# The scaled input of the projections: from x laid out twice and factors spread by matmuls, in place of transposes

## The chip, the cores and the metric

The kernel runs on one core of one Trainium2 chip. The metric is the device time of one execution in microseconds. Before the change three runs took 4046.52 to 4047.17, with a median of 4046.59.

The engines are called as in the profile: PE does matrix products and transposes, PEld is its loading of the stationary operand, DVE, ACT and POOL work on tiles element by element, and SP issues nearly all DMAs.

## The reference

One layer of a streaming encoder on 4096 tokens of 1024 features, in float32. The part that matters here is its first step, the RMS norm of the tokens and the projection:

```python
def rmsnorm(x, w):
    xf = x.astype(jnp.float32)
    y = xf * lax.rsqrt(jnp.mean(xf * xf, axis=-1, keepdims=True) + EPS)
    return (y * w.astype(jnp.float32)).astype(x.dtype)

a = rmsnorm(h, attn_norm_w[i])
proj = (a @ w_in[i]).astype(f32)          # 1024 -> 3584 columns
sb_q, sb_k, sb_v, hg_q, hg_f, hg_i, hg_g = jnp.split(proj, ...)
# blocks of 128 tokens: stick-breaking attention on sb_q, sb_k, sb_v (8 heads of 64)
# a gated linear recurrence on hg_* (4 heads of 128), out projection, residual
# routed experts, per-layer embeddings, a last RMS norm
```

Each token is divided by its own root mean square. The weights of the norm belong to features and are multiplied into `w_in`.

## The kernel before

`mix_phase` (line 162) is the first of five phases and ends its first part at some 770 us. It cuts the tokens into 16 chunks of 256 (`CH`) and works through jobs: A for chunks 0 to 15, which project v, k and q and do the attention, then B, twice over the chunks, for the recurrence. The change touches the jobs A only.

**Products.** Each fp32 product of the projections is done as three products of rounded halves (`mm3`, lines 103 to 105). Both operands are therefore split: into a rounded part `h` and the rest `l`. For the tokens these are the tiles `ATh` and `ATl`, features on partitions and tokens in the row.

**Preparation of a chunk** (`prep`, line 181). `xload` (line 178) brings x with tokens on partitions, two tiles `xin` of 128x1024. `stat` lets ACT square and sum each token (line 189), DVE works out one over the root in Newton's steps (`rsqrt_newton`, lines 66 to 74, tiles `xnr` and `xrs`), and POOL (DVE in chunk 0) multiplies the two tiles by it (line 194). Then four calls `tr(g)` each transpose four blocks of 128x128 on PE against the identity into PSUM (line 202, tile `xtp`); ACT copies that to SBUF (line 205), tile `on`; ACT makes the rounded part (line 207) and DVE the rest (line 208). The copy also goes to DRAM (`atd`, line 209), from where the jobs B read it again.

**Order.** All engines work in the order in which the code issues (the schedule is a manual one). `weave` (line 45) merges lists of steps by a position from 0 to 1 in the job. The job of chunk c has as its main list 24 steps of projections: eight for v (`tok_major`), eight for k and eight for q (`col_major`). Beside it run the attention of chunk c-1 and the preparation of chunk c+1. The table `PREP` has the positions of the latter: `stat` at 0.3 and the four `tr` at 0.5, 0.568, 0.636 and 0.704 (for chunk 1, in the first job, 0.44 and 0.62 onward). `xload` of chunk c+2 is at 0.931.

**Attention** (`attn`, line 398) goes head by head through `stage(h)`. On PE a pair of heads gets its scores (`zz`, lines 404 and 406). Then, for head h: two sigmoids on ACT (`sn` and `sp`, lines 412 and 413), a scan on DVE (line 415, `aP`), a product on POOL (line 418, `a`), a small update on DVE (line 421, `pcar`). The head two back is transposed on PE (line 427) and masked by DVE (line 429) into `aTs`, and the head three back is multiplied with v on PE (`avm`, lines 440 and 441), with `aTs` as the stationary operand. `aTs` has one buffer, `a` three, `on` two. When the keys of heads 0 and 4 begin to be projected, ACT also moves the last columns of the old keys (`carry`, line 359, `kst`).

**The start.** Before the first job, DVE and ACT split the weights of v and k (lines 150 and 151), 512 columns each, in steps of 128 features, while x and the weights come in. DVE's copy of the first results of v (line 353) stands behind these.

Of the kernel before, what the change touches and what calls it, by code (L numbers as in the profile page):

```python
# [7 lines left out]
F32 = mybir.dt.float32  # L8
# [4 lines left out]
AF = mybir.ActivationFunctionType  # L13
# [79 lines left out]
PREP = [0.3, 0.5, 0.068, 0.44, 0.62, 0.049, 0.931]  # L93
# [68 lines left out]
def mix_phase(tc, nc, x, anw, w_in, lbd, mix, qd, kd, vd, atd, C, flag, wp, atp, next_weights, filler):  # L162
    with tc.tile_pool(name="gw", bufs=1) as gw, tc.tile_pool(name="r4", bufs=3) as r4p, \
# [17 lines left out]
        def prep(c):  # L181
            st = {}

            def stat():
                ms = sm.tile([P, BPC], F32, name="xms", tag="xms")
                at = halves(atp)
                junk = at[1].rearrange("p k t -> p (k t)")
                for b in range(BPC):
                    nc.scalar.activation(junk[:, b * D:(b + 1) * D], X[c][b], AF.Square, accum_out=ms[:, b:b + 1])
                r = sm.tile([P, BPC], F32, name="xrs", tag="xrs")  # L190
                rsqrt_newton(nc, sm, r, ms, 1.0 / D, EPS, "xnr")
                eng = nc.gpsimd if c else nc.vector
                for b in range(BPC):
                    eng.tensor_scalar(X[c][b], X[c][b], r[:, b:b + 1], 0.0, op0=OP.mult, op1=OP.add)
                AT[c] = at

            def tr(g):
                ps = ptp.tile([P, 2, CH], F32, name="xtp", tag="tp")
                for j in range(2):
                    for b in range(BPC):  # L200
                        k = g * 2 + j
                        nc.tensor.transpose(ps[:, j, b * P:(b + 1) * P], X[c][b][:, k * P:(k + 1) * P], C["id"])
                tag = "on" if c else ("on", "a", "sn", "sp")[g]
                f = tm.tile([P, 2, CH], F32, name=tag, tag=tag, bufs=TB.get(tag))
                nc.scalar.activation(f, ps, AF.Copy)
                h = AT[c][0][:, 2 * g:2 * g + 2, :]
                nc.scalar.activation(h, f, AF.Copy)
                nc.vector.tensor_tensor(AT[c][1][:, 2 * g:2 * g + 2, :], f, h.bitcast(F32), op=OP.subtract)
                nc.sync.dma_start(atd[c][:, g * 512:(g + 1) * 512], f.rearrange("p k t -> p (k t)"))
            if c == 1:  # L210
                return [(PREP[3], stat)] + [(PREP[4] + PREP[5] * g, lambda g=g: tr(g)) for g in range(4)]
            return [(PREP[0], stat)] + [(PREP[1] + PREP[2] * g, lambda g=g: tr(g)) for g in range(4)]

# [30 lines left out]

        def two(t):
            return t.rearrange("p (k n) -> p k n", k=2)
        ws = {n: W.steps(n, cols[n], nw, [lambda t=t: two(t) for t in ts]) for n, ts in (("v", spare), ("k", more))}
        first[0][1]()
        for f in ws["v"][:2]:
            f()  # L250
        for _, f in first[1:]:
            f()
# [431 lines left out]
        for i, (kind, hp, c) in enumerate(jobs):  # L684
# [7 lines left out]
            if i + 1 < len(jobs):  # L692
                nk, _, n_c = jobs[i + 1]
                if nk == "A":
                    sides.append(prep(n_c))
                    if n_c + 1 < NCH:
                        sides.append([(PREP[6], lambda n_c=n_c: xload(n_c + 1))])
                else:
                    sides.append(atload(n_c, kind == "B" and i > NCH))
# [1156 lines left out]
def trunk(tc, x, p, attn_norm_w, w_in, sb_norm_w, hg_lower_bounds, hg_norm_w, w_out, ffn_norm_w, w_group_router,  # L1856
# [3 lines left out]
    with tc.tile_pool(name="dram", bufs=1, space=DRAM) as dp, tc.tile_pool(name="c", bufs=1) as cp, tc.manual_schedule():  # L1860
# [15 lines left out]
        with ExitStack() as early_e, ExitStack() as early:  # L1876
# [3 lines left out]
            with tc.tile_pool(name="AT", **right) as at1, tc.tile_pool(name="W", bufs=5, side="right") as w5:  # L1880
# [10 lines left out]
                W, mT, pre = mix_phase(tc, nc, x[0], attn_norm_w[0], w_in[0], hg_lower_bounds, mix, qd, kd, vd, atd, C, R["aflag"],  # L1891
# [35 lines left out]
```

## Time and profile before

| | |
|---|---|
| profiled execution | 4046.34 us |
| its span | 4044.6 us |
| median of three runs | 4046.59 us |
| PE busy | 3985.5 us, 99% |
| DVE, ACT, POOL busy | 68%, 46%, 21% |
| mean granted clock of PE | 0.996 of full speed |
| 375 to 425 us, a steady stretch of the jobs A: busy of 50 us | PE 49.95, DVE 35.41, ACT 30.28, POOL 12.70 |
| same stretch, mean share of the DMA engines | 0.24 |

The span goes from the first to the last instruction; the profiled execution has 1.7 us around it. Matmuls are pipelined, and their ends are modelled, so the time that one takes is best read from the starts of the next ones. In a timeline each row has the start in us from the start of the span, the duration, the engine, the line, the operation with what it writes and reads, and in brackets how long its engine sat idle before it and who ended that. "x2" or "x4" are that many instructions merged into one row; a whole fp32 product is recorded as two.

### The profile page before, as it was taken

What the parts mean: (1) busy time and instruction counts of PE and PEld (TensorE: products, weight loads), DVE (VectorE), ACT (ScalarE), POOL (GpSimd) and SP (SyncE); (2) the same over time, 40 slices, a digit from 0 to 9 for tenths busy, and PEclk for the clock granted to TensorE, in tenths of its full rate; (3) what the DMA queues carried; (4) which work ended last, traced back from release to release, by engine and by line L of the source; (5) the groups of instructions that cost most, each with busy time, mean ns of one, the idle gap of its engine ahead of it and who ended that gap; (6) DMA issues with size and microseconds to landing.
All of it is one profiled execution on the core that took longest, in us unless ns stands there. A gap on an engine that the chain in (4) does not pass through costs nothing. (4 is left out here: it accounts for less than half of the span.)

```text
span 4044.6 us, 70031 instructions
## 1 busy us (share of the span) xinstructions
PE 3985.5 (99%) x26635; PEld 3607.3 (89%) x26635; DVE 2747.5 (68%) x5871; ACT 1851.5 (46%) x3345; POOL 839.4 (21%) x1075
## 2 busy tenths in 40 slices
PE   8999999999999999999999989999999999999998
PEld 7999999999999899997888879989889999987887
DVE  6777777787777778775666656655555566657776
ACT  6666666643333333323222344545555555554443
POOL 1322222222222222220111110100000000004564
PEclk9999999999999999999999999999999999999999
DMA  4222222321211112115454486776767777776654
GB/s 151 84 84 84 84 85 85 108 60 42 61 48 56 50 40 69 45 41 196 145 162 145 149 238 196 220 215 206 228 211 236 233 239 238 224 235 246 235 212 151
DMA packets 482386, 590.33 MB, mean 146 GB/s; under 512 B 33882, under 2 KB 332890, under 8 KB 482042
## 3 DMA queue, kind: packets, MB, share of 16 engines
q1 hardware_dynamic: 459370, 510.70, 40.1%
q0 software_dynamic: 22672, 75.07, 5.2%
q8 instruction: 212, 3.47, 0.4%
q14 instruction: 132, 1.08, 0.1%
HBM read 423.86 MB, written 161.81 MB: 145 GB/s over the span
## 5 line engine op out<-in xcount | busy, mean ns | idle before, releaser
L103 PE MATMUL pj<-ATh,W 128*128 128x256 f32 x2048 | 610.0, 298 | 4.0 <-DVE v L353 4.0
L103 PE MATMUL pg<-dxth,wph 128*128 128x256 f32 (+6 forms) x2048 | 602.9, 294 | 2.0 <-ACTq L1650 2.0
L105 PE MATMUL pg<-dxth,wpl 128*128 128x256 f32 (+6 forms) x2048 | 588.7, 287 | 0.0
L104 PE MATMUL pg<-dxtl,wph 128*128 128x256 f32 (+6 forms) x2048 | 588.2, 287 | 0.0
L105 PE MATMUL pj<-ATh,W 128*128 128x256 f32 x2048 | 580.5, 283 | 0.0
L1310 DVE TENSOR_TENSOR wpl<-wraw,wph 128x2048 fp32r<-128x2048 f32 x192 | 439.3, 2289 | 207.1 <-ACT wph L1299 206.5
L104 PE MATMUL pj<-ATl,W 128*128 128x256 f32 x2048 | 579.8, 283 | 0.0
L103 PE MATMUL pj<-W,ATh 128*128 128x512 f32 x1308 | 524.0, 401 | 0.3 <-ACT mixin L1219 0.3
L104 PE MATMUL pj<-W,ATh 128*128 128x512 f32 x1308 | 510.1, 390 | 0.0
L105 PE MATMUL pj<-W,ATl 128*128 128x512 f32 x1280 | 501.0, 391 | 0.0
L103 PEld LDWEIGHTS pj<-ATh,W 128*128 128x128 f32 x2048 | 392.7, 192 | 7.8 <-issue 4.4
L104 PEld LDWEIGHTS pj<-ATl,W 128*128 128x128 f32 x2048 | 393.3, 192 | 0.1
L105 PEld LDWEIGHTS pj<-ATh,W 128*128 128x128 f32 x2048 | 392.0, 191 | 0.0
L103 PEld LDWEIGHTS pg<-dxth,wph 128*128 128x128 f32 x2048 | 385.3, 188 | 4.4 <-ACTq L1650 2.4
L104 PEld LDWEIGHTS pg<-dxtl,wph 128*128 128x128 f32 x2048 | 386.2, 189 | 1.4
L105 PEld LDWEIGHTS pg<-dxth,wpl 128*128 128x128 f32 x2048 | 386.0, 188 | 0.0
L1299 ACT ACTIVATE wph<-wraw 128x2048 fp32r<-128x2048 f32 x192 | 365.8, 1905 | 0.0
L1525 POOL DMA_INDIRECT dxr<-mnd,idx x79 | 84.9, 1074 | 1077.3 <-PE dtp L1536 1034.8
L105 PEld LDWEIGHTS pj<-W,ATl 128*128 128x128 f32 x1280 | 240.3, 188 | 53.0
L104 PEld LDWEIGHTS pj<-W,ATh 128*128 128x128 f32 x1308 | 246.4, 188 | 45.6 <-DVE W L151 0.2
L103 PEld LDWEIGHTS pj<-W,ATh 128*128 128x128 f32 x1308 | 246.3, 188 | 44.7 <-ACT mixin L1219 0.5
L418 POOL TENSOR_TENSOR a<-sp,aP 128x512 f32<-128x512 f32 x128 | 153.8, 1206 | 560.0 <-DVE pcar L421 296.7
(440 smaller groups left out, 8763.0 us busy)
## 6 DMA issues: line engine op xcount, KB each, us to landing
wraw<-in_w_exp_gate_dram SPq DMA_DIRECT2D x128, 512.0 KB, 4.1
wraw<-in_w_exp_up_dram SPq DMA_DIRECT2D x128, 512.0 KB, 5.3
wraw<-in_w_exp_down_dram SPq DMA_DIRECT2D x64, 1024.0 KB, 5.1
a<-atd SPq DMA_DIRECT2D x128, 256.0 KB, 3.1
yd<-dyo SPq DMA_DIRECT2D x108, 256.0 KB, 3.1
xin<-in_x_dram SPq DMA_DIRECT2D x32, 512.0 KB, 4.7
cxin<-in_x_dram SPq DMA_DIRECT2D x32, 512.0 KB, 7.9
h1d<-h SPq DMA_DIRECT2D x32, 512.0 KB, 3.0
```

What stands on the lines that cost most here:

```text
L103: nc.tensor.matmul(out, ph, rh, start=first, stop=False)
L104: nc.tensor.matmul(out, ph, rl, start=False, stop=False)
L105: nc.tensor.matmul(out, pl, rh, start=False, stop=last)
L418: nc.gpsimd.tensor_tensor(a, sp, pt[:, 1:513], op=OP.mult)
L1299: self.nc.scalar.activation(h, t, AF.Copy)
L1310: self.nc.vector.tensor_tensor(l, t, h.bitcast(F32), op=OP.subtract)
L1525: nc.gpsimd.indirect_dma_start(out=t, out_offset=None, in_=mnd, in_offset=bass.IndirectOffsetOnAxis(ap=idx[:, e * NB + s:e * NB + s + 1], ...
```

## The change

The host gives x a second time, as `xt`, cut into chunks with features on partitions. `xload` and the Squares stay, since the sum over a token's features is still made from the first layout. `stat` no longer multiplies x. It writes each token's factor along a row of 128: two tiles of 128x128 (identity times zero, plus the factor), on POOL, in chunk 0 on DVE. `spread_r` multiplies these on PE with the identity, two whole fp32 products, which gives the 256 factors along the row on all partitions, and ACT copies them from PSUM to SBUF. Then `scaled(g)`, four times, multiplies a quarter of `xt` by them, on POOL (in chunk 0 on DVE); ACT's rounding, DVE's subtraction and the DMA to `atd` follow as before. The factors use the halves of the second `xin` tile. `get(j)` loads the two halves of `xt`; they take turns with `xin` in the ring `r4` of three buffers.

The positions change too: `get(0)` at 0.02, `stat` at 0.2 (was 0.3), `get(1)` at 0.23, `spread_r` at 0.46, `scaled` at the old places of `tr`. In chunk 1 they are 0.3, 0.44, 0.47, 0.58 and 0.62 onward.

```diff
-PREP = [0.3, 0.5, 0.068, 0.44, 0.62, 0.049, 0.931]
+PREP = [0.02, 0.2, 0.5, 0.068]
+PREP1 = [0.3, 0.44, 0.62, 0.049]
+XLOAD = 0.931
...
+            def get(j):
+                t = r4p.tile([P, 4, CH], F32, name="xtr", tag="r4") if c else gw.tile([P, 4, CH], F32, name="xtr", tag=("s4", "ql1")[j])
+                nc.sync.dma_start(t, xt[c][:, 4 * j:4 * j + 4, :])
+                st[j] = t
...
+                st["r"], st["b"] = (X[c][1][:, j * 512:j * 512 + CH] for j in range(2))
                 eng = nc.gpsimd if c else nc.vector
                 for b in range(BPC):
-                    eng.tensor_scalar(X[c][b], X[c][b], r[:, b:b + 1], 0.0, op0=OP.mult, op1=OP.add)
+                    eng.tensor_scalar(st["r"][:, b * P:(b + 1) * P], C["id"], 0.0, r[:, b:b + 1], op0=OP.mult, op1=OP.add)
                 AT[c] = at
 
-            def tr(g):
-                ps = ptp.tile([P, 2, CH], F32, name="xtp", tag="tp")
-                for j in range(2):
-                    for b in range(BPC):
-                        k = g * 2 + j
-                        nc.tensor.transpose(ps[:, j, b * P:(b + 1) * P], X[c][b][:, k * P:(k + 1) * P], C["id"])
+            def spread_r():
+
+                ps = ptp.tile([P, CH], F32, name="xrb", tag="tp", padded_shape=[P, 512])
+                for b in range(BPC):
+                    s = slice(b * P, (b + 1) * P)
+                    nc.tensor.matmul(ps[:, s], st["r"][:, s], C["id"], start=True, stop=True)
+                nc.scalar.activation(st["b"], ps, AF.Copy)
+
+            def scaled(g):
                 tag = "on" if c else ("on", "a", "sn", "sp")[g]
                 f = tm.tile([P, 2, CH], F32, name=tag, tag=tag, bufs=TB.get(tag))
-                nc.scalar.activation(f, ps, AF.Copy)
-                h = AT[c][0][:, 2 * g:2 * g + 2, :]
+                h, l = (t[:, 2 * g:2 * g + 2, :] for t in AT[c])
+                eng = nc.gpsimd if c else nc.vector
+                eng.tensor_tensor(f, st[g // 2][:, 2 * (g % 2):2 * (g % 2) + 2, :],
+                                  st["b"].rearrange("p (o t) -> p o t", o=1).broadcast_to([P, 2, CH]), op=OP.mult)
                 nc.scalar.activation(h, f, AF.Copy)
-                nc.vector.tensor_tensor(AT[c][1][:, 2 * g:2 * g + 2, :], f, h.bitcast(F32), op=OP.subtract)
+                nc.vector.tensor_tensor(l, f, h.bitcast(F32), op=OP.subtract)
                 nc.sync.dma_start(atd[c][:, g * 512:(g + 1) * 512], f.rearrange("p k t -> p (k t)"))
...
+            a = np.ascontiguousarray(a.reshape(NCH, CH, KC, P).transpose(0, 3, 2, 1))
+            arrays["in_xt_dram"] = a
```

Three places in the new order follow. Lines are those of the file that the rows belong to, so the same operation has two numbers.

The first is in a steady chunk, on ACT and POOL, around head 6 of the attention. ACT before: the sigmoids of head 6, the copy and rounding of the first quarter, the copying of keys, the sigmoids of head 7.

```order
L412 ACTIVATE sn<-z 128x512
L413 ACTIVATE sp<-z 128x512
L205 ACTIVATE on<-xtp 128x512
L207 ACTIVATE ATh<-on 128x512
L359 ACTIVATE kst<-kst 128x2x128 x2
L412 ACTIVATE sn<-z 128x512
L413 ACTIVATE sp<-z 128x512
```

ACT now, at the same place:

```order
L431 ACTIVATE sn<-z 128x512
L432 ACTIVATE sp<-z 128x512
L220 ACTIVATE ATh<-on 128x512
L378 ACTIVATE kst<-kst 128x2x128 x2
L431 ACTIVATE sn<-z 128x512
L432 ACTIVATE sp<-z 128x512
```

POOL now, from head 5 on; before, only products of line 418 stood here. The `on` that ACT rounds is the first of the four multiplies.

```order
L437 TENSOR_TENSOR a<-sp,aP_260 128x512
L437 TENSOR_TENSOR a<-sp,aP_259 128x512
L218 TENSOR_TENSOR on<-xtr,xin 128x512
L437 TENSOR_TENSOR a<-sp,aP_260 128x512
L218 TENSOR_TENSOR on<-xtr,xin 128x512 x3
```

The source of `on` moved from a copy on ACT itself to POOL, behind the product of head 6.

The second place is on DVE in the same chunk, around head 3: the scan, the update and the mask of head 1, and Newton's steps (the first and last two of which are shown). Before:

```order
L415 SCALAR_TENSOR_TENSOR aP_272<-sn,areset 128x512
L421 TENSOR_TENSOR pcar<-pcar,aP_272 128x2
L429 TENSOR_TENSOR aTs<-aT,amask 128x512
L66 TENSOR_SCALAR xnr_v<-xms 128x2
L67 TENSOR_SCALAR xnr_i<-xnr_v 128x2
```

Now:

```order
L73 TENSOR_TENSOR xnr_t<-xnr_t,xnr_v 128x2
L74 SCALAR_TENSOR_TENSOR xrs<-xnr_t,xrs 128x2
L434 SCALAR_TENSOR_TENSOR aP_260<-sn,areset 128x512
L440 TENSOR_TENSOR pcar<-pcar,aP_260 128x2
L448 TENSOR_TENSOR aTs<-aT,amask 128x512
```

Newton's steps moved from behind head 3's scan to in front of it.

The third place is on DVE at the start, between Newton's steps for chunk 0 and the weights. Before:

```order
L194 TENSOR_SCALAR xin<-xin,xrs 128x1024 x2
L151 SCALAR_TENSOR_TENSOR W<-ATh,anw,W 128x512 x4
L208 TENSOR_TENSOR ATl<-on,ATh 128x512
L208 TENSOR_TENSOR ATl<-a,ATh 128x512
L208 TENSOR_TENSOR ATl<-sn,ATh 128x512
L208 TENSOR_TENSOR ATl<-sp,ATh 128x512
L151 SCALAR_TENSOR_TENSOR W<-ATl,anw,W 128x512 x4
```

Now:

```order
L202 TENSOR_SCALAR xin<-ident,xrs 128x128 x2
L153 SCALAR_TENSOR_TENSOR W<-ATh,anw,W 128x512 x4
L218 TENSOR_TENSOR on<-xtr,xin 128x512
L221 TENSOR_TENSOR ATl<-on,ATh 128x512
L218 TENSOR_TENSOR a<-xtr,xin 128x512
L221 TENSOR_TENSOR ATl<-a,ATh 128x512
L218 TENSOR_TENSOR sn<-xtr,xin 128x512
L221 TENSOR_TENSOR ATl<-sn,ATh 128x512
L218 TENSOR_TENSOR sp<-xtr,xin 128x512
L221 TENSOR_TENSOR ATl<-sp,ATh 128x512
L153 SCALAR_TENSOR_TENSOR W<-ATl,anw,W 128x512 x4
```

The multiplies stand between the splits on one engine, and each split of DVE needs ACT's rounding of the multiply just ahead of it.

## Rows read from the trace of the kernel before

**Rows 1.** Part 1 of the page: busy us, share of the span, instructions, by engine
```profile
PE 3985.5 (99%) x26635; PEld 3607.3 (89%) x26635; DVE 2747.5 (68%) x5871; ACT 1851.5 (46%) x3345; POOL 839.4 (21%) x1075
```
**Rows 2.** Waits of PE and its weight loads, first 770 us: total, times, longest
```profile
PE xtp L202 <- DVE xin L194: 10.5, 1, 10.5
PE pj L103 <- DVE v L353: 4.0, 1, 4.0
PE xtp L202 <- POOL xin L194: 0.9, 1, 0.9
...
PEld o L440 <- DVE aTs L429: 4.5, 14, 0.9
```
**Rows 3.** Timeline of PE in chunk 8: start, duration, engine, line, operation
```profile
428.82 0.33 PE L440 MATMUL o<-v,aTs 128*128 128x64 f32 x2
...
439.33 0.61 PE L202 MATMUL xtp<-ident,xin 128*128 128x128 f32 x4
439.70 0.36 PE L103 MATMUL pj<-ATh,W 128*128 128x256 f32 x1
...
446.28 0.33 PE L440 MATMUL o<-v,aTs 128*128 128x64 f32 x2
...
450.44 0.60 PE L202 MATMUL xtp<-ident,xin 128*128 128x128 f32 x4
450.88 0.60 PE L427 MATMUL aT<-ident,a 128*128 128x128 f32 x4
```
**Rows 4.** Timeline of PE, six whole fp32 products of 128x128 in a row
```profile
1030.42 0.39 PE L631 MATMUL o<-hvg,fqs 128*128 128x128 f32 x2
...
1031.67 0.48 PE L103 MATMUL pj<-W,ATh 128*128 128x512 f32 x1
```
**Rows 5.** Timeline of ACT in chunk 8
```profile
423.67 1.06 ACT L189 ACTIVATE ATl<-xin 128x1024 fp32r<-128x1024 f32 x1
...
438.59 0.60 ACT L412 ACTIVATE sn<-z 128x512 f32<-128x512 f32 x1
...
440.61 0.63 ACT L207 ACTIVATE ATh<-on 128x512 fp32r<-128x512 f32 x1
...
441.76 0.57 ACT L412 ACTIVATE sn<-z 128x512 f32<-128x512 f32 x1
```
**Rows 6.** Timeline of DVE in chunk 8
```profile
426.80 0.31 DVE L66 TENSOR_SCALAR xnr_v<-xms 128x2 f32<-128x2 f32 x1
...
429.19 0.69 DVE L353 COPY v<-pj 128x512 f32<-128x512 f32 x1
...
439.29 1.23 DVE L415 TENSOR_TENSOR_SCAN aP<-sn,areset 128x512 f32<-128x512 f32 x1 [0.25 <-ACT sn L412]
...
441.27 1.06 DVE L208 TENSOR_TENSOR ATl<-on,ATh 128x512 fp32r<-128x512 f32 x1
442.43 1.22 DVE L415 TENSOR_TENSOR_SCAN aP<-sn,areset 128x512 f32<-128x512 f32 x1
...
443.77 0.68 DVE L429 TENSOR_TENSOR aTs<-aT,amask 128x512 f32<-128x512 f32 x1
```
**Rows 7.** POOL: one product in chunk 8, and all of line 418 (min/median/max ns)
```profile
440.69 1.10 POOL L418 TENSOR_TENSOR a<-sp,aP 128x512 f32<-128x512 f32 x1 [3.41 <-ACT on L205]
...
L418 POOL TENSOR_TENSOR a<-sp,aP x128: 1085/1093/2091, 64.9 to 844.8; 128x512 f32<-128x512 f32 x128
```
**Rows 8.** Timeline of DVE at the start
```profile
9.59 1.42 DVE L194 TENSOR_SCALAR xin<-xin,xrs 128x1024 f32<-128x1024 f32 x2
...
13.57 0.69 DVE L208 TENSOR_TENSOR ATl<-on,ATh 128x512 fp32r<-128x512 f32 x1
...
17.35 2.74 DVE L151 SCALAR_TENSOR_TENSOR W<-ATl,anw,W 128x512 fp32r<-128x512 f32 x4
...
29.61 0.68 DVE L353 COPY v<-pj 128x512 f32<-128x512 f32 x1
```
**Rows 9.** First 12 us: length, busy by engine, PEclk, DMA share, GB/s
```profile
0.00:12.00 12.00, 1.38 (x6) 1.12 (x7) 4.70 (x18) 6.21 (x9) 2.23 (x12) 1.00 0.79 267
```

More of the change, by code (lines that the diff above doesn't have):

```diff
@@ L159, in steps, with mix_phase @@
         return st + [lambda k0=k0: (split(k0), k0 + 4 < KC and load(k0 + 4)) for k0 in ks]
-def mix_phase(tc, nc, x, anw, w_in, lbd, mix, qd, kd, vd, atd, C, flag, wp, atp, next_weights, filler):
+def mix_phase(tc, nc, x, xt, anw, w_in, lbd, mix, qd, kd, vd, atd, C, flag, wp, atp, next_weights, filler):
     with tc.tile_pool(name="gw", bufs=1) as gw, tc.tile_pool(name="r4", bufs=3) as r4p, \
@@ L207, in tr @@
                 nc.scalar.activation(h, f, AF.Copy)
-                nc.vector.tensor_tensor(AT[c][1][:, 2 * g:2 * g + 2, :], f, h.bitcast(F32), op=OP.subtract)
+                nc.vector.tensor_tensor(l, f, h.bitcast(F32), op=OP.subtract)
                 nc.sync.dma_start(atd[c][:, g * 512:(g + 1) * 512], f.rearrange("p k t -> p (k t)"))
-            if c == 1:
-                return [(PREP[3], stat)] + [(PREP[4] + PREP[5] * g, lambda g=g: tr(g)) for g in range(4)]
-            return [(PREP[0], stat)] + [(PREP[1] + PREP[2] * g, lambda g=g: tr(g)) for g in range(4)]
+            first, a, b, d = PREP1 if c == 1 else PREP
@@ L214, in atload @@
+            return [(first, lambda: get(0)), (a, stat), (a + 0.03, lambda: get(1)), (b - 0.04, spread_r)] + \
+                [(b + d * g, lambda g=g: scaled(g)) for g in range(4)]
         def atload(c, early):
@@ L243, in mix_phase @@
         more = [p.tile([P, 1024], F32, name=n, tag=n) for p, n in ((l4, "l4"), (l6, "l6")) for _ in range(2)]
+        first[0][1]()
         def two(t):
             return t.rearrange("p (k n) -> p k n", k=2)
-        ws = {n: W.steps(n, cols[n], nw, [lambda t=t: two(t) for t in ts]) for n, ts in (("v", spare), ("k", more))}
-        first[0][1]()
+        ws = {}
+        for n, ts in (("v", spare), ("k", more)):
+            ws[n] = W.steps(n, cols[n], nw, [lambda t=t: two(t) for t in ts])
+            if n == "v":
+                first[2][1]()
+        first[1][1]()
         for f in ws["v"][:2]:
             f()
-        for _, f in first[1:]:
+        for _, f in first[3:]:
             f()
@@ L696, in mix_phase @@
                     if n_c + 1 < NCH:
-                        sides.append([(PREP[6], lambda n_c=n_c: xload(n_c + 1))])
+                        sides.append([(XLOAD, lambda n_c=n_c: xload(n_c + 1))])
                 else:
@@ L1890, in next_weights @@
                     return W.steps(("out", n), [wo[:, :, n * 512:(n + 1) * 512]], sc, raws)
-                W, mT, pre = mix_phase(tc, nc, x[0], attn_norm_w[0], w_in[0], hg_lower_bounds, mix, qd, kd, vd, atd, C, R["aflag"],
+                W, mT, pre = mix_phase(tc, nc, x[0], xt, attn_norm_w[0], w_in[0], hg_lower_bounds, mix, qd, kd, vd, atd, C, R["aflag"],
                               wp, atp, next_weights, (em, range(0, 4)))
@@ L1921 @@
         args.append(nc.dram_tensor(f"in_{name}_dram", a.shape, mybir.dt.from_np(a.dtype), kind="ExternalInput").ap())
+        if name == "x":
+            a = np.ascontiguousarray(a.reshape(NCH, CH, KC, P).transpose(0, 3, 2, 1))
+            arrays["in_xt_dram"] = a
+            args.append(nc.dram_tensor("in_xt_dram", a.shape, mybir.dt.from_np(a.dtype), kind="ExternalInput").ap())
     args.append(nc.dram_tensor("out_0_dram", (1, T, D), F32, kind="ExternalOutput").ap())
```

2 lines of the change are left out of this document (1 added, 1 removed).

## The prediction

> **What bounds the kernel now.** I read part 1 of the page first: PE is busy for 99% of the span [rows 1]. Then the waits of PE over the first 770 us, the only part that the change touches: in the steady chunks next to none, at the start 10.5 us for the first scaled rows, 4.0 us for DVE's copy of v, and 0.9 us for POOL's scaling in the first chunk [rows 2]. So PE's own work sets the pace of this phase, and an instruction taken from PE is worth its time, as long as nothing that PE waits for becomes later. The second question is therefore how much room lies before each thing that PE takes from others. The timelines of ACT, DVE and POOL in one steady chunk give that [rows 5 to 7]; the chunk shown is the one that projects chunk 8, finishes the attention of chunk 7 and prepares chunk 9. All 14 chunks that do these three things are alike. The median of the runs before, 4046.59, is 0.25 us above the profiled execution, 4046.34 (a span of 4044.6 and 1.7 us around it); I add to the latter.
>
> **What PE saves.** Four groups of four transposes go from each of 15 chunks. A group between a run of products and a transpose of the attention takes 450.44 to 450.88, 0.44 us; one behind a product with v takes 439.33 to 439.70, 0.37 us [rows 3]. Two of the four are of either kind: 1.62 us. In their place come two whole fp32 products of 128x128; six of these take 1030.42 to 1031.67, 1.25 us [rows 4], so two cost 0.42. 15 x (1.62 - 0.42) = 18.0 us saved. In the first chunk all of the 16 ran while DVE set the pace (below), and nothing is counted. The weight load of the product with v waits for DVE in 14 chunks, 4.5 us together [rows 2]; POOL's 1024-wide scaling, which held up DVE's scan there, is gone, and part of this wait lies beside PE's work before it: 0.2 of the 0.3 us a chunk, 2.8 us saved. The 0.9 us for POOL's scaling goes too, since the first factors are now made 0.14 of a chunk ahead of their use.
>
> **What it puts in PE's way.** In the new order POOL's multiply stands between two attention products, ACT's split waits for it, and behind ACT's split stand the next sigmoids. I follow it in the clock of before; the two new products shift PE and this chain alike. POOL's product of head 6 ends at 440.69 + 1.10 = 441.79 [rows 7]. The new multiply has its shape, with one operand repeated: 1.10 us more, 442.89. ACT's split can start at 442.95 with a handover; before it started at 440.61 [rows 5], so 2.34 us later. All behind it moves by this: sn of head 7 (441.76 before), the scan (442.43), and the masked transpose aTs of head 5, which began at 443.77 and took 0.68 [rows 5, 6]. It now ends at 443.77 + 2.34 + 0.68 = 446.79. PE asked for it at 446.28 [rows 3], and with two groups of transposes gone ahead of it (0.37 + 0.44) asks at 445.47. So the room of 1.8 us (446.28 less 444.45) becomes a wait of 1.32, 1.36 with the handover. Behind PE's waiting product stand all projections of this chunk, so it is paid in full: 14 x 1.36 = 19.0 us. The bounds: no product of line 418 took under 1.09 us and the longest took 2.09 [rows 7], which would make the wait 2.4; if the weight load hides some of the restart it is 1.1. I take the median's.
>
> The second wait is further ahead in the chunk. The two Squares move in front of head 3's sigmoids, a pair that takes ACT 1.1 us (two of 0.6, overlapped) [rows 5], so the statistics start 1.1 us earlier: 426.80 becomes some 424.8, when the Squares, begun at 423.67 - 1.1, are read out [rows 5, 6]. But DVE now does Newton's steps, 2.3 us (426.80 to 429.19 less a first step that was held up) [rows 6], ahead of head 3's scan instead of behind aTs of head 1. The scan starts at 427.1, aTs 1.34 us later (as 442.43 to 443.77) and ends 0.68 later, at 429.15 [rows 6]. POOL's two writes of factors fall between scan and aTs; a POOL operation beside a DVE one that reads two tiles costs DVE up to the rest of that operation (the split at 441.27 took 1.06 beside POOL's product, 0.69 at 13.57 with POOL idle) [rows 6 to 8]; they are an eighth as wide as the old scaling, so I add 0.2. PE asks at 428.82 [rows 3]: a wait of 0.5, bounds 0.2 and 0.9, 14 x 0.5 = 7.0 us.
>
> The second split precedes aTs of head 6. Head 7's scan ends at 442.43 + 2.34 + 1.22 = 445.99, its product begins 0.17 behind that (440.69 against 439.29 + 1.23) and takes 1.10, the second multiply at 448.4, ACT's split (0.63) at 449.1, DVE's (0.69) at 449.8, aTs at 450.4 [rows 5 to 8]. PE, having waited, asks 4.2 us after 446.83 (446.28 to 450.88 and another 0.44, less two groups [rows 3]), at 451.0. That leaves 0.6, or 0.3 when POOL's third multiply holds up DVE's split; the third and fourth leave about as much before head 7's. I add 0.1 a chunk for both, 1.4 us, with bounds of 0 and 0.6. ACT loses four copies a chunk and gains a smaller one; it is idle for a third of a chunk, and this hides. The transposed x, 1 MB a chunk, comes in on SP's queue while the DMA engines are mostly idle (the table above), long ahead of its use, and costs nothing.
>
> **The start.** Here DVE sets the pace: it works without a gap from 9.59 to the copy of v at 29.61, for which PE waits [rows 2, 8]. Before, its four splits took 13.57 to 17.35, 3.8 us [rows 8]. Now each is multiply, wait for ACT, split, in one queue: 0.69 + 0.63 + 0.69 [rows 5, 8] with handovers less overlaps, 1.95 us, four times 7.8: 4.0 us later. Half of the transposed x, 0.5 MB, is loaded ahead of the first weights, 2.0 us at the 267 GB/s of these 12 us [rows 9]; 1.2 us of it is paid by the scaling that DVE no longer does (1.42 against two writes an eighth as wide) [rows 8]. Between 0 and 0.8, I take 0.4. The copy of v is late by 4.4 us and PE with it, bounds 3 and 6.
>
> **Sum.** -18.0 - 2.8 - 0.9 + 19.0 + 7.0 + 1.4 + 4.4 = +10.1: 4046.3 + 10.1 = 4056.4, I say 4056.5, slower by 0.25%. With the waits, the later splits and the start all at their low ends it is 4046, at their high ends some 4085; all ends together are unlikely, and 4048 to 4066 is this case's own range.
>
> **The rivals.**
> PE's work alone decides: the chains keep enough room, no new wait appears. For it: PE's 99%, and ACT and DVE have idle time in every steady chunk. Against it: the room of 1.8 us before head 5's product is less than the 2.34 that POOL's multiply and the lost transposes' 0.81 take from it. Time: 4046.3 - 21.7 + 4.4 = 4029. This decides if POOL's multiply and its handovers take under 0.3 us, or ACT finds the sigmoids ready first, which the order forbids.
>
> The gain is just eaten: the waits are there but near their low ends (1.0 and 0.2), since the weight load hides their start. 4056.4 - 14 x 0.66 - 1.4 = 4046, no change to be measured.
>
> The port is the mechanism, and more of it: POOL now has five multiplies and products in a row beside DVE's splits, which read two tiles, each waiting for the whole of the other. Where POOL's third multiply begins just ahead of a split, the split and aTs of head 6 behind it are up to 1.1 us late; against 0.3 of room, and half of the times, that is 0.4 to 0.6 a chunk more. 4056.4 + 14 x 0.6 = about 4065. For it: 1.06 against 0.69 in rows 6 and 8. Against it: POOL waits for buffers between its multiplies, which spreads them.
> The Trainium skill (SBUF — State Buffer, section "Who interferes with whom") states it as an exclusive lock: a DVE instruction with two SBUF inputs and a GpSimd instruction that reads SBUF do not run together, the later one blocks fully. The split at 441.27 fits: POOL was done at 441.79, and 0.69 from there ends at 442.48, measured 442.33.
>
> **How the numbers follow.** The forecast has a chance of 0.58, the port's 0.14, the eaten gain 0.15, PE alone 0.13. A measurement of this kernel can tell about 0.2%, 8.1 us, from no change: 4038.2 to 4054.4. About two thirds of the forecast's own range lie above this. Slower: 0.38 + 0.14 = 0.52; same: 0.20 + 0.15 = 0.35; faster: 0.13. The range for 8 in 10 goes from 4040, with the eaten gain whole, to 4070.
>
> **What would show it.** PE waiting for aTs in its products with v, some 1.4 us at head 5 and 0.5 at head 1 in each of 14 chunks; POOL's first multiply ending before ACT's split begins at once; a steady chunk longer by 0.6 us or so; the copy of v at 34 instead of 29.6. The forecast is wrong if a chunk becomes shorter, if PE waits for another thing than aTs, or if the start is late by under 3 us.

## The result and the profile after

The changed kernel takes 4072.89 us (median of four runs, 4070.90 to 4075.35) against 4046.88 us: a ratio of 1.0066, 95% interval 1.0054 to 1.0077, slower by 26 us. The direction was forecast, the size was not: +10.1 us and a range up to 4070. The profiled execution is the longest of the four, 4075.35 us with a span of 4073.5, 28.9 above the span before.

Part 1 of the page after, as [rows 1]: busy us, share of the span, instructions.

```profile
PE 3983.2 (98%) x26443; PEld 3594.2 (88%) x26443; DVE 2757.2 (68%) x5875; ACT 1817.7 (45%) x3297; POOL 897.6 (22%) x1135
```

PE has 192 instructions less and is busy only 2.3 us less, though the transposes taken away were worth far more: part of its work ran at a lower clock (a mean granted clock of 0.994 against 0.996). And it waits. The waits of PE over the whole span (total us, times, longest) answer to [rows 2]:

```profile
PE o L459 <- DVE aTs L448: 25.5, 32, 3.2
PE xrb L210 <- DVE xin L202: 9.8, 1, 9.8
...
PE pg L105 <- DMA dxr<-mnd,idx: 6.1, 1, 6.1
...
PE pj L105 <- DVE v L372: 4.0, 1, 4.0
```

25.5 us for the masked transposes stand where 1.0 us stood. One steady chunk shows how they arise. PE's timeline in chunk 6 (start, duration, engine, line, operation, idle time and its end), as [rows 3]:

```profile
338.25 0.43 PE L459 MATMUL o<-v,aTs 128*128 128x64 f32 x2 [0.31 <-DVE aTs L448]
...
342.12 0.60 PE L446 MATMUL aT<-ident,a 128*128 128x128 f32 x4
342.56 0.33 PE L459 MATMUL o<-v,aTs 128*128 128x64 f32 x2
342.73 0.39 PE L460 MATMUL o<-v,aTs 128*128 128x64 f32 x2
...
354.90 0.60 PE L446 MATMUL aT<-ident,a 128*128 128x128 f32 x4
356.56 0.43 PE L459 MATMUL o<-v,aTs 128*128 128x64 f32 x2 [1.06 <-DVE aTs L448]
356.83 0.39 PE L460 MATMUL o<-v,aTs 128*128 128x64 f32 x2
...
360.42 0.60 PE L446 MATMUL aT<-ident,a 128*128 128x128 f32 x4
361.03 0.43 PE L459 MATMUL o<-v,aTs 128*128 128x64 f32 x2
```

The starts tell more than the brackets. Head 2 is undisturbed: 0.44 us from its transposes to its product. Head 5 takes 1.66, and its first two products 0.27 instead of 0.17: a stall of 1.32 us, of which the bracket shows 1.06. Head 6 has no bracket at all, yet takes 0.61. The same stretch on POOL, ACT and DVE, one view each, as [rows 5 to 7]:

```profile
350.35 1.09 POOL L437 TENSOR_TENSOR a<-sp,aP 128x512 f32<-128x512 f32 x1 [3.54 <-DVE aP L434]
351.40 1.28 POOL L218 TENSOR_TENSOR on<-xtr,xin 128x512 f32<-128x512 f32 x1
...
356.92 2.90 POOL L218 TENSOR_TENSOR on<-xtr,xin 128x512 f32<-128x512 f32 x2
```

```profile
352.72 0.63 ACT L220 ACTIVATE ATh<-on 128x512 fp32r<-128x512 f32 x1 [3.38 <-POOL on L218]
...
353.87 0.58 ACT L431 ACTIVATE sn<-z 128x512 f32<-128x512 f32 x1
```

```profile
354.48 1.23 DVE L434 TENSOR_TENSOR_SCAN aP<-sn,areset 128x512 f32<-128x512 f32 x1 [0.41 <-ACT sn L431]
...
355.82 0.68 DVE L448 TENSOR_TENSOR aTs<-aT,amask 128x512 f32<-128x512 f32 x1
356.54 2.13 DVE L398 TENSOR_TENSOR kst<-sn,kst 64x256 fp32r<-64x256 f32 x2
359.08 1.29 DVE L221 TENSOR_TENSOR ATl<-on,ATh 128x512 fp32r<-128x512 f32 x1 [0.42 <-ACT ATh L220]
```

This is the predicted chain, link by link: product of head 6, multiply, split, sigmoid of head 7, scan, masked transpose of head 5, PE. ACT had nothing else to do for 3.38 us, and the sigmoids stood behind its waiting split.

Chunk 3, in which the level masks are made, is another case. POOL's timeline there, and then PE's:

```profile
201.46 0.15 POOL L310 MEMSET on<- 128x64 f32 x1 [1.62 <-DVE hgm L318]
...
206.31 1.26 POOL L218 TENSOR_TENSOR on<-xtr,xin 128x512 f32<-128x512 f32 x1 [2.63 <-DVE hgm L318]
```

```profile
209.62 0.43 PE L459 MATMUL o<-v,aTs 128*128 128x64 f32 x2 [3.25 <-DVE aTs L448]
...
211.21 0.28 PE L107 MATMUL pj<-ATh,W 128*128 128x256 f32 x1
211.33 0.35 PE L105 MATMUL pj<-ATh,W 128*128 128x256 f32 x1
211.48 0.42 PE L106 MATMUL pj<-ATl,W 128*128 128x256 f32 x1
211.70 0.42 PE L107 MATMUL pj<-ATh,W 128*128 128x256 f32 x1
```

Masks and multiplies take turns in the two buffers of "on" (`TB` gives it no more), and the fourth multiply waits until DVE has copied a mask out. PE stands for 3.25 us, and 1.7 us after it resumes, equal products come every 0.21 us instead of 0.12. Stretches of the changed kernel by length, busy us of PE, PEld, DVE, ACT and POOL, granted clock, DMA share, GB/s:

```profile
209.00:215.00 6.00, 5.38 (x33) 5.39 (x34) 3.45 (x8) 4.36 (x10) 0.00 (x0) 0.72 0.15 51
...
375.00:425.00 50.00, 48.63 (x367) 45.84 (x366) 35.58 (x75) 27.32 (x61) 16.64 (x14) 1.00 0.29 102
175.00:225.00 50.00, 45.36 (x340) 43.13 (x339) 32.83 (x81) 27.29 (x61) 17.09 (x26) 0.97 0.22 75
425.00:475.00 50.00, 47.24 (x340) 44.24 (x339) 32.44 (x65) 25.91 (x57) 16.36 (x14) 0.97 0.30 103
```

Steady stretches keep the full clock; the stretches with chunk 3 and chunk 8 do not. In chunk 8 the same fourth multiply is late, this time for a store from the ring, by the turns of two buffers that of the second multiply (POOL's timeline, and below it one line of the DMA view of 460 to 467 us):

```profile
465.60 1.29 POOL L218 TENSOR_TENSOR on<-xtr,xin 128x512 f32<-128x512 f32 x1 [3.30 <-DMA atd<-on]
```

```profile
q8 instruction: 1, 0.02, 1.8%
```

In the steady chunk that wait is 1.07. The second line is one transfer of 16 KB by the queue that the page calls "instruction", while the store was under way; more of it below, at e18_after32. PE stalls for 1.40 us in chunk 8, and from 468 to 476 us its granted clock is 0.79. So a long stall is paid twice, once as a wait and once as slow work behind it.

**Where the 28.9 us are.** From the starts of each chunk's first score product in PE's timeline: up to the first one +1.3; a steady chunk 51.23 against 50.43, fourteen times +0.80 makes 11.2; chunk 3 takes 56.31 against 51.01, 4.5 beyond that; chunks 8 to 10 take 54.37, 53.02 and 51.38, 5.1 beyond; everything behind the attention +6.9.

### The profile page after: what moved, and what is told of

Read it like the earlier page. It is cut to its first block, busy times and chain, and to the rows that moved or that the text cites. A ratio compares the mean times of both kernels' runs of the same rounds, so it can differ in the third digit from the quotient of the medians.

```text
span 4073.5 us, 69659 instructions
## 1 busy us (share of the span) xinstructions
PE 3983.2 (98%) x26443; PEld 3594.2 (88%) x26443; DVE 2757.2 (68%) x5875; ACT 1817.7 (45%) x3297; POOL 897.6 (22%) x1135
## 4 chain that ended last, share of the span: by engine, by line
PE 51%; DMA 1%; DVE 1%; issue 0%; ACT 0%; POOL 0%; POOLq 0%; DVEq 0%; ACTq 0%
PE pg L107 6%; PE pg L105 6%; PE pg L106 6%; PE pj L105 6%; PE pj L107 6%; PE pj L106 6%; PE pdn L105 3%; PE pdn L106 3%; PE pdn L107 3%; PE dtp L1555 2%; PE etp L1770 1%; PE mtp L993 1%; PE ctp L914 1%; PE pdn L1608 1%; PE pdn L1610 0%
## 5 line engine op out<-in xcount | busy, mean ns | idle before, releaser
L1558 DVE SCALAR_TENSOR_TENSOR dxtl<-dtp,dfn,dxth 128x256 fp32r<-128x256 f32 (+6 forms) x256 | 125.5, 496 | 208.7 <-ACT dxth L1557 208.6
```

Of the source, the lines that this page charges most:

```text
L1558: nc.vector.scalar_tensor_tensor(l[:, k, 0:n], ps[:, 0:n], fn[:, k:k + 1], h[:, k, 0:n].bitcast(F32), op0=OP.mult, op1=OP.subtract)
```

## The experiments

In the table "steady" is the usual distance of these score products (to 0.02), "chunk 3" that of chunk 3, "others" what further chunks lie above steady in all, "attention" the time from the first of them to the first product of the level matrices, all from one profile each. The ratio is to the kernel before, run beside it at 4043.7 to 4046.9; times of different rows are compared by it.

| kernel | median us | ratio, 95% | steady | chunk 3 | others | attention |
|---|---|---|---|---|---|---|
| before | 4046.88 | 1 | 50.43 | 51.01 | 0 | 787.3 |
| changed | 4072.89 | 1.0066 (1.0054 to 1.0077) | 51.23 | 56.31 | 5.1 | 808.0 |
| e9_after_again | 4068.95 | 1.0060 (1.0046 to 1.0073) | 51.24 | 57.41 | 2.4 | 805.9 |
| e8_before_xt | 4049.59 | 1.0013 (1.0003 to 1.0022) | 50.41 | 51.00 | 0 | 786.8 |
| e5_nomul | 4039.35 | 0.9990 (0.9981 to 0.9999) | 49.62 | 49.87 | 0 | 775.3 |
| e1_stat | 4060.59 | 1.0044 (1.0030 to 1.0057) | 50.66 | 55.48 | 2.6 | 797.3 |
| e2_late | 4042.52 | 1.0000 (0.9991 to 1.0009) | 49.65 | 53.16 | 0.2 | 778.4 |
| e3_dve | 4074.66 | 1.0075 (1.0061 to 1.0089) | 51.87 | 54.58 | 0.7 | 810.1 |
| e4_inplace | 4063.80 | 1.0050 (1.0036 to 1.0064) | 51.22 | 52.04 | 0.4 | 798.9 |
| e16_masks | 4066.35 (one) | - | 51.25 | 51.47 | 3.1 | 801.5 |
| e7_both_inplace | 4062.58 | 1.0045 (1.0032 to 1.0059) | 50.75 | 50.03 | 3.0 | 792.9 |
| e10_both_ring | 4036.90 | 0.9980 (0.9971 to 0.9989) | 49.07 | 52.32 | 0.9 | 773.0 |
| e11_both_masks | 4031.60 | 0.9971 (0.9960 to 0.9982) | 49.07 | 49.20 | 0 | 767.5 |
| e13_both_dve | 4045.28 | 1.0003 (0.9994 to 1.0012) | 49.80 | 50.87 | 1.4 | 779.6 |
| e17_best32 | 4031.48 | 0.9967 (0.9955 to 0.9979) | 49.07 | 49.20 | 0 | 767.4 |
| e18_after32 | 4069.66 | 1.0064 (1.0051 to 1.0078) | 51.25 | 56.31 | 2.9 | 805.2 |

**The changed kernel again, and the kernel before with the added input.**

> The changed kernel once more, on the chip of these runs. Theory: about 26 us above the kernel before, of which 22 in the chunks of the attention: steady chunk 51.23, chunk 3 near 56, chunks 8 to 10 long again by 5 us in all because the order of the ring puts them so. Rival (chunks 8 to 10 come from the state of the DMA engines in that one execution): other chunks are long, or none, and the total is 4 to 6 us lower.

The steady chunk repeats, and chunk 3 nearly. Chunks 8 and 9 are long again, by 2.4 us together where the first profile had 5.1 in chunks 8 to 10. In chunk 8 PE's stall was 0.93 us and not 1.40, and the granted clock from 468 to 476 us was 1.00 and not 0.79. That the order alone sets the place of these chunks looks right here, but does not hold: e18_after32, with the same order in them, has its long ones elsewhere (below).

```
+ nc.sync.dma_start(pcar..., xt[0][:, 0, 0:NH * BPC])   # kernel before, one corner of xt
```

> The kernel before with the transposed x as an added input of which one 8 KB corner is loaded and never used. It measures the part of the loss that lies behind the attention's chunks (from the first level product to the end 3184 us before, 3191 after, 3187 to 3189 in the four other variants). Theory (the added input, by where it puts the other arrays, costs time in the later phases): 4 to 7 us more than the kernel before, with a longer wait for the gather dxr. Rival (it comes with the code of the change or varies from run to run): no change, within 2 us of the kernel before.

Five us more in the median, of which 4.0 are at the start in the profile (the first score product at 64.6 instead of 60.6, behind the added transfer). The theory's time came, but not for its reason: PE's wait ahead of the experts is 2.18 us, as before (1.99), and everything behind the attention is 3.3 us shorter than before, in the one profile. So the input by itself does not make the +6.9.

**The multiply left out.**

```
- eng.tensor_tensor(f, st[g // 2][...], st["b"]..., op=OP.mult)   # chunks 1 to 15
+ f = st[g // 2][...]
```

> The changed kernel without the four multiplies of chunks 1 to 15 (the split takes the loaded transposed x as it is, unscaled; the spread products and the copy of the factors stay). It measures what the change is worth with POOL's multiplies away. Theory (the multiplies make the loss: head 5's wait, the ring, the port): PE keeps its saving of 18 us and the start costs 1.3, head 1's wait stays at 5 to 7: 4035 to 4049, faster than or like the kernel before, steady chunk 50.0 or less. Rival (PE's saving is smaller than counted, or the wait is ACT's order and not the multiply): over 4055, with PE still waiting at head 5.

No wait at head 5, none in chunks 8 to 10, chunk 3 within 0.25 us of the others: the multiply makes all three, together with its place in the ring, which went with it. The 0.3 us of head 1 stay.

**The statistics put back.**

```
- PREP = [0.02, 0.2, 0.5, 0.068]
+ PREP = [0.02, 0.3, 0.5, 0.068]
```

> The changed kernel with the statistics of the next chunk back at 0.3 of a chunk (behind head 3's sigmoids, where the kernel before had them); all else of the change stays. Theory: Newton's steps no longer stand ahead of head 3's scan, so PE's wait in head 1's product (0.31 us shown, 0.54 at its weight load, some 0.1 of restart) goes in each of 14 chunks: 4 to 8 us less than the changed kernel, some 4067, and the steady chunk 0.3 to 0.5 us shorter than 51.23. Rival (the loss sits at the multiplies alone, and PE only loses at head 5 what it saves at head 1): no change, 4073, and head 5's wait grows by what head 1's lost.

The chunk is 0.57 shorter (0.5 was predicted, 0.31 shown in the bracket), and the kernel is 16.9 us above the kernel before, where the changed one is 24.5 to 26.0. Head 5's wait is unchanged at 1.04. The rival falls.

**The multiplies moved behind head 7's sigmoids.**

```
- PREP = [0.02, 0.2, 0.5, 0.068]
+ PREP = [0.02, 0.2, 0.575, 0.05]
```

> The changed kernel with its four multiplies and their splits moved from 0.5, 0.568, ... to 0.575, 0.625, 0.675, 0.725 of a chunk, that is behind head 7's sigmoids instead of ahead of them. Theory: ACT's split no longer stands in front of head 7's sigmoids, so the chain multiply, split, sigmoid, scan, masked transpose that head 5's product waits for is cut; 14 x (1.06 + restart) = some 15 us less than the changed kernel, 4058. Rival 1 (port and DVE's queue: the splits only move ahead of the masked transposes of heads 6 and 7, each held up by a POOL multiply): the wait turns up there, under 5 us gained, 4068 to 4073. Rival 2 (too few products are left in the chunk for four splits): the next chunk's first products wait for the split and it is slower than the changed kernel.

1.58 us a chunk come back, the whole loss in time: four positions of one table (the spreading products move with them, from 0.46 to 0.535). The theory's 15 us were too few: a steady chunk gave back heads 6 and 7 as well, 22 us in all, chunks 8 to 10 another 4.9 and chunk 3 1.6.

**The multiplies on DVE.**

```
- eng = nc.gpsimd if c else nc.vector      # in scaled()
+ eng = nc.vector
```

> The changed kernel with its multiplies on DVE instead of POOL in chunks 1 to 15, nothing moved. Theory (the chain's price is POOL's 1.28 to 1.46 us behind its product of head 6, and the port): the multiply costs 0.69 and need not wait for POOL, head 5's stall falls from 1.32 to about 0.5 and the later ones (0.27) go: steady chunk 50.1 to 50.5, chunk 8 as the others, total 4050 to 4056. Rival (the order decides, whoever multiplies: ACT's split stands ahead of head 7's sigmoids, and DVE now waits for ACT in front of head 7's scan): 51 or more, 4065 to 4075.

The rival was right: with POOL's four multiplies gone, and with them what they cost DVE beside them, the chunk is longer, 51.87. PE now waits at three heads:

```profile
340.22 0.43 PE L459 MATMUL o<-v,aTs 128*128 128x64 f32 x2 [0.30 <-DVE aTs L448]
...
357.90 0.43 PE L459 MATMUL o<-v,aTs 128*128 128x64 f32 x2 [0.43 <-DVE aTs L448]
...
367.42 0.43 PE L459 MATMUL o<-v,aTs 128*128 128x64 f32 x2 [1.28 <-DVE aTs L448]
```

Head 5's wait shrinks from 1.06 to 0.43, since the multiply needs no longer wait for POOL's product; a larger one turns up later, behind DVE's queue of multiply, wait for ACT, split, 0.70 us idle each time. At this place in the order DVE is no better than POOL.

**The ring.**

```
- f = tm.tile([P, 2, CH], F32, name=tag, tag=tag, bufs=TB.get(tag))
+ f = x2 if c else tm.tile(...)            # x2: this quarter of the loaded xtr
```

> The changed kernel with the multiply writing into the loaded transposed x itself (chunks 1 to 15) instead of into the ring of two buffers 'on', which it shares with the level masks, the head norms and its own stores. Theory: the three odd chunks of the changed kernel come from that ring (chunk 3, where POOL's masks wait for DVE's copies: 56.0 us against 51.0; chunks 8 to 10, where the fourth multiply waits for the first's store: 3.5, 1.4 and 0.2 above 51.23): chunk 3 becomes 4 to 5 us shorter, 8 and 9 as the others, together 8 to 9 us less, 4064; the steady chunk stays at 51.2. Rival (these chunks are odd because of the granted clock or the DMA engines, the ring's wait is a symptom): under 4 us gained, 4069 to 4073, and a chunk near the ninth is still long.

Chunk 3 falls to 52.04, chunks 8 to 10 are as the others, the attention is 9.1 us shorter. The steady chunk does not move. The theory holds. What makes the store late in just these chunks is a question of its own (below).

```
- sides.append([(0.1 + 0.1 * i + 0.08 * j, m[j]) ...
+ sides.append([(0.02 + 0.07 * i + 0.055 * j, m[j]) ...
```

> The changed kernel with nothing moved but the level masks of chunk 3 (built at 0.02 to 0.37 instead of 0.1 to 0.6). Theory: chunk 3 falls from 56.3 to 51.2 to 52.0, as with the multiply in place (52.0), and the chunks 8 to 10 stay long by 2 to 5 us in all, since they have no masks; one execution at 4063 to 4068. Rival (POOL's mask builds cost chunk 3 the time wherever they stand): chunk 3 stays over 54.

The masks alone free chunk 3, in one execution; the odd chunks without masks stay.

**Everything together, and a surprise.** e6_both and e7_both_inplace are one kernel, with the multiply in place; the first gave 4060.48 us (ratio 1.0041). The first expectation is for the kernel with the ring, which is e10_both_ring below.

> The changed kernel with both moves: statistics back at 0.3 of a chunk, multiplies at 0.575, 0.625, 0.675, 0.725. Theory: both waits of PE for the masked transposes are gone and what is left is what PE saves; the chunk falls from 49.65 (multiplies moved alone) to 49.1 to 49.25, since head 1's wait (0.3 us shown and a restart) goes; 14 x 0.4 = 6 us below the run with the multiplies moved alone, 4036, faster than the kernel before by 7. Rival (PE's saving is 0.8 a chunk and head 1's wait lies beside other work): steady chunk 49.6, 4042, like the kernel before.

> As the run with both moves, and the multiply writes into the loaded transposed x instead of the ring 'on'. Theory: chunk 3 with the level masks, 53.2 us with the multiplies moved alone, comes to within 1 us of the others; 2.5 to 3.5 us below the run with both moves, 4033, the fastest so far. Rival (the ring no longer matters once the multiplies lie behind head 7's sigmoids): no difference to the run with both moves.

The second expectation failed: chunk 3 came near the others (50.03), but the time did not. Two moves, each good, and the buffer wait removed gave 50.75 a chunk, 1.1 us more than the multiplies moved alone. POOL, DVE and PE in one chunk of e7_both_inplace, a view each:

```profile
395.93 5.84 POOL L219 TENSOR_TENSOR xtr<-xtr,xin 128x512 f32<-128x512 f32 x4
```

```profile
396.38 2.54 DVE L399 TENSOR_TENSOR kst<-sn,kst 64x256 fp32r<-64x256 f32 x2 [0.88 <-ACT kst L398]
398.95 3.37 DVE L222 TENSOR_TENSOR ATl<-xtr,ATh 128x512 fp32r<-128x512 f32 x2
402.24 0.68 DVE L449 TENSOR_TENSOR aTs<-aT,amask 128x512 f32<-128x512 f32 x1
```

```profile
402.97 0.44 PE L460 MATMUL o<-v,aTs 128*128 128x64 f32 x2 [1.42 <-DVE aTs L449]
```

With a place for each result POOL runs four multiplies without a pause, to 401.77. Beside it DVE's kst row takes 2.54 us, where the next one, with POOL idle, takes 0.87, and the splits take 3.37; the masked transpose behind them starts only when POOL is done.

```
- f = x2 if c else tm.tile(...)
+ f = tm.tile([P, 2, CH], F32, name=tag, tag=tag, bufs=TB.get(tag))   # as in the change
```

> The changed kernel with both moves (statistics at 0.3, multiplies at 0.575, 0.625, 0.675, 0.725) and the multiply writing into the ring 'on' as the change has it; the runs e6_both and e7_both_inplace were one and the same kernel, with the multiply in place. Theory (the ring of two makes POOL pause between the second and third multiply, in place it does all four in one go, 5.84 us, and DVE's splits beside it take 3.37 for two): with the ring the chunk is free of the 1.42 us wait of the in-place runs, and of head 1's: 49.05 to 49.15 us, 49.65 less 0.57; 4034 to 4038, faster than the kernel before by 6 to 10. Rival (the statistics at 0.3 crowd the multiplies themselves): 50.7 as in place, 4060.

With the ring the same multiplies come in two pairs, and DVE gets between them (POOL, then DVE, of e10_both_ring):

```profile
390.37 2.70 POOL L218 TENSOR_TENSOR on<-xtr,xin 128x512 f32<-128x512 f32 x2
395.44 2.86 POOL L218 TENSOR_TENSOR on<-xtr,xin 128x512 f32<-128x512 f32 x2 [2.37 <-DVE aTs L448]
```

```profile
393.39 1.29 DVE L221 TENSOR_TENSOR ATl<-on,ATh 128x512 fp32r<-128x512 f32 x2
394.60 0.68 DVE L448 TENSOR_TENSOR aTs<-aT,amask 128x512 f32<-128x512 f32 x1
```

The two splits that took 3.37 us take 1.29, the masked transpose is in time, and the chunk is 49.07, as expected. The pause of this chunk, 2.37 us, is a long one; in most it is 1.1 to 1.4, and the splits fit as well. The two kernels differ in the ring alone: the wait for a buffer that cost chunk 3 so much is what keeps POOL off DVE in the others.

> As e10_both_ring, and the six level masks of chunk 3 are built from 0.02 to 0.37 of the chunk (copies to 0.43) instead of from 0.1 to 0.68, so that none shares the ring 'on' with a multiply. Theory (chunk 3 is long because masks and multiplies take turns in the ring): chunk 3, 53.2 us with the multiplies moved alone, comes to within 0.8 of the others, 2.5 to 3.5 us below e10_both_ring. Rival (the masks cost their time by POOL and the port wherever they stand, as the kernel before lost 0.6 by them): no difference, or new waits in the heads 0 to 4.

Chunk 3 joins the others at 49.20, and PE waits once for a masked transpose, 0.4 us, in the stretch from 100 to 800 us. Its stretches show the room used up:

```profile
375.00:425.00 50.00, 49.95 (x382) 47.74 (x382) 38.18 (x78) 29.70 (x65) 16.73 (x14) 1.00 0.32 110
175.00:225.00 50.00, 50.00 (x380) 47.63 (x380) 41.53 (x89) 31.53 (x67) 20.22 (x22) 1.00 0.30 107
```

This version is faster than the kernel before by 0.29% (0.18 to 0.40), 12 us: the change pays once its steps stand elsewhere.

> Both moves and the multiplies on DVE. Theory (without POOL there is no lock, and DVE has a quarter of each chunk free): PE's saving is whole, 49.05, chunk 3 shorter than with POOL; like e10_both_ring or up to 3 us less, 4032 to 4038. Rival (four times multiply, wait for ACT's split, split in DVE's one queue holds up the masked transposes of heads 5 to 7, as at the start of the kernel, 1.95 us each): a wait of 0.5 to 1.5 us in each chunk, 4042 to 4056.

On DVE the same order has a wait of about 0.5 us a chunk and is no faster than before: the rival. POOL is the right place, if it is given pauses.

**What lies behind the attention.** In the changed kernel PE's first product of the experts, behind a branch that all engines pass, waits 6.1 us, and in e11_both_masks 4.85; before it was 1.99. PE's timeline there, of before, and then of e11_both_masks:

```profile
2371.44 0.42 PE L103 MATMUL pg<-dxth,wph 128*128 128x336 f32 x1 [1.99 <-ACTq L1650]
2371.70 0.32 PE L104 MATMUL pg<-dxtl,wph 128*128 128x336 f32 x1
```

```profile
2354.52 0.62 PE L105 MATMUL pg<-dxth,wph 128*128 128x336 f32 x1 [4.85 <-DMA dxr<-mnd,idx]
2354.94 0.48 PE L106 MATMUL pg<-dxtl,wph 128*128 128x336 f32 x1
```

```
+ for _ in range(48):   # 16 in e15_pad64; first chunk, of no use
+     nc.tensor.matmul(pad[:, 0:8], C["id"], C["id"][:, 0:8], start=True, stop=True)
```

> e11_both_masks with 192 more PE instructions (96 fp32 products of 8 columns, of no use) at the start, so that PE issues 26635 as the kernel before. They cost some 5 to 20 us at the start, which does not count here. Theory (PE fetches its code at the branch in front of the experts, and how long that takes hangs on where the branch falls in its stream): PE's first product of the experts waits about 2.0 us as in the kernel before and not 4.85, and its next ones take 0.32 and not 0.48 us. Rival (another engine's stream, or the order of the transfers, which this leaves as the change made them): the wait stays at 4.8 to 6.4.

> As e14_pad192 with 64 more PE instructions instead of 192. Theory (position in PE's stream): a wait between 2 and 6.4 that differs from both others; with the rival it stays at 4.8 to 6.4 as in e11_both_masks.

These small products count once, so PE had 96 and 32 instructions more (26539 and 26475). With 96 the wait was 5.85 us, with 32 it was 2.31, and the products behind it took 0.31: nothing but PE's own stream had changed, so it has a share in the wait. That it is the place of the branch in the stream is likely, but not shown. Single executions: 4040.43 and 4026.43 us.

> The kernel of e15_pad64 once more, which had 32 more PE instructions than e11_both_masks (the small products counted once each, and the two runs with them added 96 and 32, not 192 and 64). Theory: the wait ahead of the experts is 2.3 us again and the kernel is 3 to 6 us below e11_both_masks, whose ratio to the kernel before was 0.9971: 0.9956 to 0.9964 here. Rival (the one look was a lucky execution): 0.997.

> The changed kernel with the same 32 PE instructions of no use in its first chunk and nothing else. Theory: the wait ahead of the experts falls from 6.10 to 2.0 to 2.4 us and the products behind it run at 0.31 instead of 0.48 us; 4 to 6 us less than the changed kernel, a ratio to the kernel before of 1.0047 to 1.0056 where the changed kernel had 1.0066 and 1.006. Rival (another wait takes its place): 1.006, no change.

The shorter wait repeats: 2.35 us in the first, with the short products behind it, and 3.91 in the second, where the products turn long at the sixth. The time does not follow: 4031.48 is e11_both_masks' 4031.60, and 1.0064 is within the interval of the changed kernel. Whether something later takes it back is not shown. From there to the last phase's first transpose the profile of e17_best32 has 1276.8 us, against 1275.6 in e11_both_masks and 1275.2 before, but e15_pad64, the same kernel as e17_best32, has 1274.2, so single executions of one kernel differ here by 2.6 us.

e18_after32 shows something else. Its long chunks are 13 and 14 (52.30 and 52.61), and chunk 8, at 51.23, is as the others, though nothing in these chunks was changed. POOL's fourth multiply in chunk 14, and a line of the DMA view of the 4 us ahead of its start:

```profile
774.09 1.29 POOL L222 TENSOR_TENSOR on<-xtr,xin 128x512 f32<-128x512 f32 x1 [3.02 <-DMA atd<-on]
```

```profile
q8 instruction: 1, 0.02, 2.7%
```

In five profiles with the multiplies at the changed places (the changed kernel twice, e1_stat, e16_masks, e18_after32) six chunks in a row have such a 16 KB instruction transfer in these 4 us: chunks 4 to 9, and 9 to 14 with the 32 added instructions. In the last two of the six POOL waits 2.4 to 3.3 us ahead of its fourth multiply, in the first four 1.05 to 1.31, and in chunks without a transfer 1.05 to 1.14 (chunk 3 with its masks aside). So the place of the odd chunks goes with the place of these transfers, which the added PE instructions moved. Why only the last two delay the store is not shown.

## Why the prediction was right or wrong

- **What PE saves** (18.0, and 2.8 for the freed wait: 1.40 a chunk): right. With all new waits gone the chunk is 49.07 against 50.43, 1.36. The 0.9 us for POOL's factors was wrong, the first chunk still waits 0.89 for them. The rival that PE alone decides, 4029, a ratio of 0.9957, is what e11_both_masks comes near to (0.9971), not the change as it stands.
- **Head 5** (1.36): right, 1.32 by the starts, though POOL's multiply is slower than the product it was priced by: 1.26 us at the least and 1.46 in the middle of 60, not 1.10. Here it took 1.28, and PE asked 4.99 us behind the start of POOL's product of head 6 where 4.78 was worked out. The two nearly cancel: that the sum comes out to 0.04 is partly luck.
- **Head 1** (0.5): right, 0.57 by e1_stat, 0.58 between e2_late and e10_both_ring.
- **The start** (+4.4): the copy of v starts at 33.29 instead of 29.61, 3.7 late and within its bounds, each multiply with its split taking the 2.0 us worked out. But by the first score product only 1.3 of it are left. 1.2 are the transposes of chunk 1, which stood there too; the rest fits the granted clock, from 24 to 60 us 0.91 before and 0.95 after, 1.4 us of the 36 by an estimate from these shares. In e9_after_again, at 0.97, nothing is left (60.52 us, before 60.58). DVE's timeline at the start, as [rows 8]:

```profile
13.06 0.69 DVE L218 TENSOR_TENSOR on<-xtr,xin 128x512 f32<-128x512 f32 x1
14.45 0.69 DVE L221 TENSOR_TENSOR ATl<-on,ATh 128x512 fp32r<-128x512 f32 x1 [0.70 <-ACT ATh L220]
15.05 0.69 DVE L218 TENSOR_TENSOR a<-xtr,xin 128x512 f32<-128x512 f32 x1
...
33.29 0.67 DVE L372 COPY v<-pj 128x512 f32<-128x512 f32 x1
```

- **The step that failed** is "All 14 chunks that do these three things are alike", by which every wait was multiplied by 14, and with it the price of the second split and those behind it, "I add 0.1 a chunk for both, 1.4 us, with bounds of 0 and 0.6". In the steady chunk these heads cost 0.27 (50.66 in e1_stat less 49.07 and head 5's 1.32), 3.8 us in all and within the bounds. In chunk 3 and chunks 8 to 10 they cost 9.6 more. The kernel before already had chunk 3 at 51.01 against 50.43. I counted POOL's wait for buffers between its multiplies only as something that spreads them, against a rival; that the ring is shared with the masks and with the multiply's own stores, that PE's stall then grows past 3 us, and that its clock falls behind it, was not priced. e4_inplace takes 9.1 us of the attention's loss away.
- **A second step that failed** is "the first 770 us, the only part that the change touches". The 6.9 us behind the attention were put at nothing. In the profile 3.8 of them lie up to PE's first product of the experts, where the wait is 4.1 longer, and 3.1 between there and the last phase, 2.4 of these in the first 40 products (8.69 us against 6.26). e9_after_again has 6.5, the other kernels with the multiplies 7.1 (e3_dve) to -0.6 (e15_pad64). PE's own stream has a share, by the runs with added instructions; the rest of the cause stays open.
- **Together**, against the +10.1 of the forecast, the +28.9 of the profile differs by +9.6 in the odd chunks, +6.9 behind the attention, +3.4 in the steady chunks (11.2 against 7.8 worked out), and -1.0 up to the first score product (1.3 against 2.3).
- **The port**: not what makes most of the loss as the change stands (e3_dve, without POOL's multiplies, is slower still). In the steady chunk it has head 6's 0.27 us at most, against the rival's 0.4 to 0.6: DVE's split at 359.08 took 1.29 us beside POOL's multiplies instead of 0.69, and the masked transpose of head 6 stands behind it. One step further it is decisive. The Trainium skill (SBUF — State Buffer, section "Who interferes with whom") calls it an exclusive lock of DVE and GpSimd on one shared pair of ports. The trace of e7_both_inplace agrees as far as it shows: two splits in 3.37 us beside the multiplies, 1.29 in e10_both_ring, and a masked transpose that starts 0.47 us after POOL's last one ends.

## What to carry to other kernels

Before work is taken from the busiest engine, ask what the replacement stands in front of: here a wait ahead of the sigmoids cost more than the transposes had, and four positions in a table turned 26 us of loss into 12 of gain together with two others. A shared ring of two buffers is a schedule too: look in every chunk that differs for who else uses it, and before removing its wait ask whom it holds back. Read a stall from the starts of the instructions around it, since the bracket shows only part of it (1.06 of 1.32, 0.31 of 0.57).

## What the runs showed of the hardware

- After a stall of 3.25 us PE ran at full rate for 1.7 us, then equal products took 0.21 us instead of 0.12, with a granted clock of 0.72 over those six us; after 4.85 us at the branch they were slow at once (0.48 against 0.32), after 3.91 in e18_after32 from the sixth on.
- A multiply of 128x512 on POOL with one operand repeated took 1.26 us or more where a product of two full tiles of that size took 1.09.
- 32 more instructions in PE's stream, some 2300 us ahead of a branch, changed the wait there from 4.85 to 2.3 us, 96 more to 5.85.
- All ten waits of 2.4 to 3.3 us of POOL's fourth multiply, with a store from the ring of two under way, had a 16 KB instruction transfer in their last 4 us; without one the wait was 1.05 to 1.14. Twenty such transfers went by with 1.05 to 1.31.
